# A two-layer hybrid decoder on one core: the RWKV recurrence worked in units of two pairs of heads instead of one

## Chip, core and metric

One core of a Trainium2 chip runs the whole program. The metric is the device time of one execution in microseconds (us). The engines are called as in the profile: PE (TensorE matmuls; PEld its weight loads), DVE (VectorE), ACT (ScalarE), POOL (GpSimd) and SP (SyncE, which here issues all DMAs, in order).

## The reference, cut to what matters

Two layers over 512 tokens of width 1024. Each layer projects x with one wide matrix and feeds four branches of width 512 (RWKV-7 time mixing, latent attention, a convolution module, attention into 256 memory tokens); each is gated, projected, merged with sigmoid gates, and a normalized residual closes the layer. The change lies in the RWKV branch:

```python
kk = heads(k * k_k); kk = kk / max(norm(kk), 1e-12)
k  = k * (1.0 + (a - 1.0) * k_a)
...
def step(state, inp):
    r_t, w_t, k_t, v_t, a_t, b_t = inp          # a = -kk, b = kk * a
    sa = einsum('bhvk,bhk->bhv', state, a_t)
    state = state * w_t + sa (x) b_t + v_t (x) k_t
    return state, einsum('bhvk,bhk->bhv', state, r_t)
_, y = lax.scan(step, s0, xs)                   # 512 steps, 8 heads x 64
y = (y - y_mu) * rsqrt(y_var + 64e-5) * lnx_g + lnx_b + bonus
```

## The kernel before

**Order of the work.** No order is written by hand. `Plan` (L67) keeps a clock for each engine from formulas of its own for each operation's cost, and emits the instructions in the order in which generators become due. A stream of "items" (the projections: 128-row matmuls, each product made of three from a high and a low half of both operands) is PE's main line; side tasks step in between. Tasks that wait for "small" matmuls (64 by 64) are taken together: the planner waits until GATHER (L28, 3000 ns) after the last such group, then lets every waiting small task run before it goes back to 128-row matmuls. The engines then run what was emitted, in order, waiting on semaphores for data. All engine calls go through L231, matmuls through L282, transposes through L287, DMAs through L294, so that tile names, not lines, tell the operations apart.

**Weights.** Blocks of 512 KB come by SP's queue, at most two raw ones at a time (WR); ACT rounds each half (`w..h`), DVE makes the rest (`w..l`).

**The recurrence** (`rwkv_unit`, L711). The scan is done in chunks of 64 tokens as matrix products. A unit is one pair of heads `j` (128 channels on the partitions) and one half `hf` of the 512 tokens, so four chunks for two heads: eight blocks of 64 by 64. There are 16 units, eight in each layer. The steps of a unit, by their tile names:

- `zw` (PE, 128 rows), `th`, `ta`, `cum` (scan on DVE), `kk`, `sq`, `D`, `E`, `bt`, `w`, `AR`: decays, keys and queries scaled;
- `g` (small matmuls): products of `bt` and `AR`, and the squared norms; from these `rn` and, with one scalar instruction for each of four blocks, the strictly triangular `M`; `Mc` gathers M's 16 by 16 diagonal blocks with the mask `bm`, and `moff` then clears them in M;
- `substitution()`: `Mc` goes to DRAM and comes back as `W`, one 16 by 16 block for each of 32 partitions; 30 POOL instructions invert the blocks into `ZT`; that goes to DRAM and comes back as `tc`, `zq`, `zc`;
- meanwhile `kt`, `bo` (the bonus), and `gk` (three sets of eight small matmuls, and six transposes into a second tile);
- `T`, `Zd`, `Q` spread the inverted blocks with the mask `bm` on DVE, then four small steps assemble the inverse: `x0` (needs T), `x1` (needs Zd), `x2`, `va`;
- `gb` (state updates `Gs`, `H`, and `B`, `Y0`), three `w` steps that carry the state `S` from chunk to chunk, and `yb`, the output;
- group normalization of `yb` (bn_stats, `gr` by POOL, four subtract-and-scale on DVE), transposes `ty`, and `yr`.

In the profile the digit after x is left out, so `x<-T,M` is x0 and `x<-QQ,PP` is x2.

**What overlaps.** Up to the bonus a unit may run while the unit before is still in its substitution (the conditions on `L["mids"]`, `L["toks"]`, `L["front"]`); from `gk` on, units follow each other. Two fronts, and a front and a middle, are so in flight at once, with tiles in two or three buffers. The units of a pair start when its r, k and v are there. The RWKV gate `rg` for pair i is ready when `L["units"] >= 2 * i + 2`.

Of the kernel before, what the change touches and what calls it, by code (L numbers as in the profile page):

```python
# [27 lines left out]
GATHER = 3000.0  # L28
# [18 lines left out]
for _n, _c in _PARTS:  # L47
# [6 lines left out]
    ("minc", 64), ("moff", 64), ("bm", 4), ("id2", 64),  # L54
# [148 lines left out]
class Engine:  # L203
# [5 lines left out]
    def __getattr__(self, name):  # L209
        f = getattr(self.eng, name)  # L210

        def call(*a, **k):
# [5 lines left out]
            if self.key == "ACT":  # L218
                c = (65 if isinstance(k.get("scale", 0.0), (int, float)) else 270) + 0.83 * n
            elif self.key == "POOL":  # L220
                c = 200 + 167 * n if k.get("op") == ALU.pow else 250 + 1.6 * n
            elif name == "scalar_tensor_tensor":
                c = 100 + 1.07 * n
# [38 lines left out]
def trunk_kernel(ctx: ExitStack, tc: tile.TileContext, A, out, dbg=None):  # L262
# [82 lines left out]
    scr = [[dp.tile([32 * (n + 1), 256], F32, tag=f"scr{n}{i}", name=f"scr{n}{i}").rearrange("a b -> (a b)") for n in range(2)] for i in range(2)]  # L345
# [9 lines left out]
    dpads = [cp.tile([128, 4, 65], F32, tag=f"dpad{i}", name=f"dpad{i}") for i in range(3)]  # L355
# [238 lines left out]
    def layer_items(l):  # L594
# [62 lines left out]
        def begin_rwkv(get):  # L657
# [6 lines left out]
            L["blk"] = [L["rp"].tile([32] + n, F32, tag=x, name=x + t_) for x, n in (("W", [16, 16]), ("ZT", [2, 16, 16]), ("tmpW", [56]))]  # L664
# [26 lines left out]
        def q3(ap, c=4):  # L691
            return ap.rearrange("p (c v) -> p c v", c=c)

        def rk2(tag, name, shape, bufs=1):
            return L["rp"].tile([128] + shape, F32, tag=tag, name=name, bufs=bufs)

        state = [None] * 4
        L["yr"] = [None] * 4
        L["units"] = L["chains"] = L["toks"] = L["mids"] = L["subs"] = L["next"] = L["read"] = 0
        L["front"] = False  # L700
# [8 lines left out]
        quads = [(cp, c2, h) for cp in range(2) for c2 in range(2) for h in range(2)]  # L709

        def rwkv_unit(j, hf, r, k, v):  # L711
            t = f"_{l}_{j}_{hf}"
            un = 2 * j + hf
            cs = slice(256 * hf, 256 * hf + 256)
            rr, kr, vr = r[:, cs], k[:, cs], v[:, cs]
            jc = slice(128 * j, 128 * j + 128)
            om = PRM[l][2]

            def rt(name, tag=None, dt=F32, bufs=1):
                return L["rp"].tile([128, 256], dt, tag=tag or name, name=name + t, bufs=bufs)  # L720

            def chunks(ap):

                return ap.rearrange("p (a b) w -> p b a w", b=2)

            def by2(ap):
                return ap.rearrange("p (a b) w -> p a b w", a=2)

            z, = yield from pa.take([128, 2, 256], "zw" + t)
            for i, (h, lo, x) in enumerate(L["lora"]):  # L730
                MM(z[:, i, :], h[:, jc], x[:, cs], start=True, stop=False)
                MM(z[:, i, :], lo[:, jc], x[:, cs], start=False, stop=True)
            yield
            th, ta = rt("th"), rt("ta")
            S.activation(th, z[:, 0, :], AF.Tanh, scale=0.5, bias=hp("w0", j))
            S.activation(ta, z[:, 1, :], AF.Tanh, scale=0.5, bias=hp("a0", j))
            pa.free()
            V.tensor_scalar(out=th, in0=th, scalar1=1.0, scalar2=KAPPA, op0=ALU.add, op1=ALU.mult)
            yield
            cum = rt("cum")  # L740
            V.tensor_tensor_scan(out=cum, data0=reset, data1=th, initial=0.0, op0=ALU.mult, op1=ALU.add)
            kk, sq = rt("kk"), rt("sq")
            S.activation(sq, kr, AF.Square, scale=pr("k_k", j))
            S.activation(kk, kr, AF.Copy, scale=pr("k_k", j))
            yield
            D = dpads[un % 3]
            S.activation(D[:, :, 1:65], q3(cum), AF.Exp, scale=-1.0)
            E = rt("E", "th")
            S.activation(E, cum, AF.Exp)
            yield lambda: L["toks"] >= un - 1  # L750
            bt, kt, w = rt("bt", bufs=2), rt("kt", bufs=2), rt("w")
            V.scalar_tensor_tensor(out=bt, in0=ta, scalar=1.0, in1=kk, op0=ALU.add, op1=ALU.mult)
            V.scalar_tensor_tensor(out=bt, in0=bt, scalar=0.5, in1=E, op0=ALU.mult, op1=ALU.mult)
            S.activation(w, ta, AF.Identity, scale=hp("k_a", j), bias=om[:, 13 + j:14 + j])
            yield
            yield lambda: L["mids"] >= un - 1
            AR = rk2("AR", "AR" + t, [4, 2, 64], 2)
            V.scalar_tensor_tensor(out=AR[:, :, 0, :], in0=q3(kk), scalar=-1.0, in1=D[:, :, 0:64], op0=ALU.mult, op1=ALU.mult)
            V.tensor_tensor(out=AR[:, :, 1, :], in0=q3(rr), in1=D[:, :, 1:65], op=ALU.mult)
            yield  # L760

            yield lambda: L["subs"] == un
            g0, = yield from pg.take([128, 2, 512], "g" + t, 1, "small")
            for cp, c2, h in quads:
                c = 2 * cp + c2
                MM(g0[HALF[c2], h, 64 * cp:64 * cp + 64], bt[HALF[h], 64 * c:64 * c + 64], AR[HALF[h], c, 0], start=True, stop=True, four=True)
            for cp, c2, h in quads:
                c = 2 * cp + c2
                MM(g0[HALF[c2], h, 128 + cp:129 + cp], sq[HALF[h], 64 * c:64 * c + 64], bones2[HALF[h], h:h + 1], start=True, stop=True, four=True)
            yield  # L770
            s1, rn = st("s1" + t, 4), rk2("rn", "rn" + t, [4], 3)
            V.tensor_scalar(out=s1.rearrange("p (a b) -> p a b", a=2), in0=g0[:, :, 128:130], scalar1=1e-24, scalar2=None, op0=ALU.max)
            V.reciprocal(rn[:, 0:4:2], s1[:, 0:4:2])
            V.reciprocal(rn[:, 1:4:2], s1[:, 3:0:-2])
            M = rk2("M", "M" + t, [4, 64], 2)
            for h in range(2):
                for cp in range(2):
                    e = 2 * (h ^ cp) + cp
                    V.scalar_tensor_tensor(out=M[:, e, :], in0=g0[:, h, 64 * cp:64 * cp + 64], scalar=rn[:, e:e + 1], in1=cc("mstr"), op0=ALU.mult, op1=ALU.mult)
            pg.free()  # L780
            bm = cc("bm")
            Mc = rk2("Mc", "Mc" + t, [4, 16])
            V.tensor_scalar(out=Mc, in0=M[:, :, 0:16], scalar1=bm[:, 0:1], scalar2=None, op0=ALU.mult)
            for b in range(1, 4):
                V.scalar_tensor_tensor(out=Mc, in0=M[:, :, 16 * b:16 * b + 16], scalar=bm[:, b:b + 1], in1=Mc, op0=ALU.mult, op1=ALU.add)
            V.tensor_tensor(out=M, in0=M, in1=cc("moff").unsqueeze(1).to_broadcast([128, 4, 64]), op=ALU.mult)
# [5 lines left out]
            def substitution():  # L792
# [3 lines left out]
                DMA(d1.rearrange("(c p t) -> p c t", c=4, t=16), Mc)  # L796
                plan.due(d1)
                yield
                DMA(W.rearrange("p a b -> p (a b)"), d1.rearrange("(q e) -> q e", q=32), "W" + t)
# [6 lines left out]
                for q in range(1, 15):  # L806
                    n = 15 - q
                    o = tmp[:, 0:q * n].rearrange("p (a b) -> p a b", a=q)
                    G.tensor_tensor(out=o, in0=zz[:, 0:q, q:q + 1].to_broadcast([32, q, n]),
                                    in1=W[:, q:q + 1, q + 1:16].to_broadcast([32, q, n]), op=ALU.mult)  # L810
# [6 lines left out]
                DMA(d2.rearrange("(z q e) -> q z e", z=2, q=32), ZT.rearrange("p z a b -> p z (a b)"))  # L817
                plan.due(d2)
                yield
                zc, tc_, zq = (rk2(n, n + t, [4, 16], 1 + (n != "zq")) for n in ("zc", "tc", "zq"))  # L820
                dz, dt = (d2[4 * 128 * 16 * i:4 * 128 * 16 * (i + 1)] for i in range(2))
                DMA(tc_, dt.rearrange("(e p t) -> p e t", e=4, t=16))
                DMA(zq, dz.rearrange("(e p t) -> p e t", e=4, t=16))
                dz = dz.rearrange("(h c p t) -> h p c t", h=2, c=4, t=16)
                for h in range(2):
                    DMA(zc[HALF[h]], dz[h])
# [5 lines left out]
            V.tensor_tensor(out=w, in0=w, in1=kr, op=ALU.mult)  # L832
            V.tensor_tensor(out=kt, in0=w, in1=E, op=ALU.mult)
            yield
            rbh, rbl = rt("rbh", "kk", F32R), rt("rbl", "ta", F32R)
            V.scalar_tensor_tensor(out=w, in0=rr, scalar=pr("r_k", j), in1=w, op0=ALU.mult, op1=ALU.mult)
            yield from split(rbh, rbl, w)
            yield
            bo, = yield from pa.take([128, 256], "bo" + t)
            MM(bo, bones, rbl, start=True, stop=False)  # L840
            MM(bo, bones, rbh, start=False, stop=True)
            yield
            yield lambda: L["units"] >= un - 2
            bon = rk2("bon", "bon" + t, [256], 3)
            V.tensor_tensor(out=bon, in0=bo, in1=vr, op=ALU.mult)
            pa.free()
            L["front"] = False


            yield lambda: L["mids"] == un  # L850
# [190 lines left out]
        def room():  # L1041

            return min(adds[0:8]) > 0
# [915 lines left out]
```

## Time and profile before

| | before |
|---|---|
| time, median of 3 runs | 1540.28 us (1539.13 to 1546.58) |
| the profiled execution, as timed | 1538.63 us |
| its span, first to last instruction | 1536.5 us |
| PE busy | 1508.7 us, 98% of the span |
| DVE, ACT, POOL busy | 1123.2, 650.1, 238.1 us |
| instructions, all engines | 30218 |
| DMA bytes, busy share of the 16 engines (queue q1) | 151.61 MB, 32.7% |
| granted clock of PE | 0.997 |

The profile is one execution. A row of a timeline is start, duration, engine, line, operation, output and inputs, for PE the rows by columns of the array, the moving size, and how many instructions it stands for; a 64 by 64 matmul in float32 is two of them. A row of a stretch gives its length, then the busy us (and instructions) of PE, PEld, DVE, ACT and POOL, the granted clock, the DMA share and GB/s. A group's row ends in busy us, mean ns, and the idle time before. PE's matmuls are pipelined, so the distance of two starts, not a duration, is what a matmul costs PE.

### The profile page before, as it was taken

The numbers are of one execution on the slowest core, as the hardware profiler recorded it, in microseconds if no ns is written. First come the engines' busy times: TensorE is split into PE (matmuls) and PEld (weight loads), VectorE is DVE, ScalarE is ACT, GpSimd is POOL, SyncE is SP. The second block draws the span as 40 slices with busy tenths as digits, with TensorE's granted clock in tenths as the row PEclk, the third lists the DMA queues.
The fourth block names the chain that finished last, engine by engine and source line by source line (L and its number), as shares of the span: only waits on it lengthen the run. The fifth ranks groups of instructions, "written<-read, shape, count | busy, mean of one in ns | idle before, by whom it ended". The sixth has DMA issues, their size and how long they took to land.

```text
span 1536.5 us, 30218 instructions
## 1 busy us (share of the span) xinstructions
PE 1508.7 (98%) x11912; PEld 1239.7 (81%) x11912; DVE 1123.2 (73%) x2503; ACT 650.1 (42%) x1403; POOL 238.1 (15%) x588
## 2 busy tenths in 40 slices
PE   8999999999999999999999999999999999999997
PEld 8878788877787777888998877788777777778886
DVE  5789888888657775455554888887977777745747
ACT  5546654443234332344365454534423533323332
POOL 0000000345214330000000000000534333300002
PEclk9999999999999999999999999999999999999998
DMA  6452422232322232424343243332222222326231
GB/s 207 122 163 70 117 83 83 78 89 64 90 82 78 61 96 83 147 97 137 113 154 107 80 121 91 86 110 87 76 76 76 66 77 75 95 78 205 96 113 66
DMA packets 89662, 153.54 MB, mean 100 GB/s; under 512 B 41648, under 2 KB 47792, under 8 KB 89520
## 3 DMA queue, kind: packets, MB, share of 16 engines
q1 hardware_dynamic: 89520, 151.61, 32.7%
q8 instruction: 93, 1.52, 0.4%
q14 instruction: 49, 0.40, 0.1%
HBM read 134.27 MB, written 5.77 MB: 91 GB/s over the span
## 4 chain that ended last, share of the span: by engine, by line
PE 85%; DVE 7%; DMA 3%; ACT 2%; issue 1%; POOL 0%; SPq 0%; ACTq 0%; DVEq 0%; POOLq 0%
PE ps_m L282 22%; PE po L282 11%; PE ps_cg L282 3%; PE ps_rg L282 3%; PE ps_k L282 3%; PE ps_xg L282 3%; PE ps_v L282 3%; PE ps_xq L282 3%; PE ps_r L282 3%; PE ps_mg L282 3%; PE ms L282 2%; PE ps_glu L282 2%; PE pz L282 2%; PE pl L282 2%; PE ps_val L282 2%; DMA w<-in_w_ch_dram 2%
## 5 line engine op out<-in xcount | busy, mean ns | idle before, releaser
L231 DVE SCALAR_TENSOR_TENSOR cacc<-hpad,prm,cacc 128x512 f32<-128x512 f32 x240 | 179.7, 751 | 3.3
L231 ACT ACTIVATE tm<-ps_m,prm 128x512 f32<-128x512 f32 x64 | 44.1, 689 | 135.1 <-PE ps_m L282 135.0
L231 POOL TENSOR_SCALAR ZT<-W 32x256 f32<-32x256 f32 x16 | 7.3, 457 | 562.5 <-DMA W<-scr 320.9
L231 DVE SCALAR_TENSOR_TENSOR mt<-tm,po 128x512 f32<-128x512 f32 x48 | 33.0, 687 | 77.5 <-PE po L282 77.5
L231 POOL TENSOR_TENSOR ZT<-ZT,tmpW 32x14 f32<-32x14 f32 (+6 forms) x224 | 85.1, 380 | 17.6
L231 POOL TENSOR_TENSOR tmpW<-ZT,W 32x14 f32<-32x14 f32 (+6 forms) x224 | 85.0, 379 | 15.9
L231 POOL TENSOR_SCALAR lrs<-lmv 128x1 f32<-128x1 f32 x8 | 1.7, 206 | 302.1 <-DVE lmv L231 302.1
L231 POOL TENSOR_SCALAR gr<-gm 128x4 f32<-128x4 f32 x16 | 5.5, 343 | 262.3 <-DVE gm L231 262.3
L231 ACT ACTIVATE mP<-ms,nmm 128x128 f32<-128x128 f32 (+3 forms) x64 | 33.6, 527 | 19.4 <-DVE nmm L231 16.7
L231 DVE TENSOR_TENSOR merged<-merged,mt 128x512 f32<-128x512 f32 x48 | 33.7, 702 | 1.7
L231 DVE TENSOR_REDUCE nmm<-ms 128x1 f32<-128x128 f32 (+3 forms) x64 | 30.3, 485 | 0.8 <-PE ms L282 0.3
L231 ACT COPY mPT<-mt 128x128 f32<-128x128 f32 (+3 forms) x64 | 26.2, 430 | 11.1 <-PE mt L287 10.7
L231 DVE SCALAR_TENSOR_TENSOR S<-w,dpad,H 128x64 f32<-128x64 f32 x48 | 13.5, 281 | 22.8 <-PE w L282 22.6
L287 PE MATMUL mt<-cst,mP 128*128 128x128 f32 x160 | 27.0, 277 | 1.1 <-DVE smm L231 0.7
L231 DVE TENSOR_SCALAR mP<-mP,smm 128x128 f32<-128x128 f32 (+3 forms) x64 | 24.8, 387 | 2.3
L282 PE MATMUL mo<-mPT,v 128*64 128x128 f32 x320 | 24.3, 282 | 0.0
L231 ACT ACTIVATE xP<-xs,nmx 128x256 f32<-128x256 f32 x32 | 15.2, 475 | 21.3 <-DVE nmx L231 21.0
L287 PEld LDWEIGHTS mt<-cst,mP 128*128 128x128 f32 x160 | 18.8, 141 | 6.7 <-issue 1.0
L231 ACT ACTIVATE z<-z,lnb,lrs 128x256 f32<-128x256 f32 (+1 forms) x16 | 9.6, 648 | 30.8 <-DVE lnb L231 30.8
L282 PE MATMUL ms<-kTl,qT 96*128 96x128 f32 (+3 forms) x64 | 22.5, 352 | 0.0
L282 PEld LDWEIGHTS mo<-mPT,v 128*64 128x64 f32 x320 | 16.8, 136 | 5.3 <-issue 3.1
L282 PE MATMUL ms<-kTh,qT 96*128 96x128 f32 (+3 forms) x64 | 20.6, 323 | 0.0
(3516 smaller groups left out, 5424.4 us busy)
## 6 DMA issues: line engine op xcount, KB each, us to landing
w<-in_w_ch_dram SPq DMA_DIRECT2D x146, 512.0 KB, 3.8
w<-in_w_o_dram SPq DMA_DIRECT2D x32, 512.0 KB, 3.7
w<-in_w_out_dram SPq DMA_DIRECT2D x16, 512.0 KB, 3.8
w<-in_w_lat_dram SPq DMA_DIRECT2D x16, 336.0 KB, 3.0
w<-in_w_mk_dram SPq DMA_DIRECT2D x8, 512.0 KB, 3.7
w<-in_w_mv_dram SPq DMA_DIRECT2D x8, 512.0 KB, 3.7
w<-in_w_qk_dram SPq DMA_DIRECT2D x8, 320.0 KB, 2.9
x<-in_xT_dram SPq DMA_DIRECT2D x8, 256.0 KB, 6.3
```

The source lines that it names most:

```text
L231: return self.plan.keep(f(*a, **k))
L282: plan.keep(nc.tensor.matmul(o, lhsT, rhs, start=start, stop=stop))
L287: plan.keep(nc.tensor.transpose(o, i, ident))
```

## The change

A unit becomes two neighbouring pairs of heads (s = 0, 1) and one half of the tokens: 8 units in all, four in each layer. Every step is done for both: each small step has the sets of both pairs in one go, DVE and ACT instructions take 512 columns where the operands allow (L707 to L1060 of the new kernel), the substitution has 64 partitions of blocks and transfers twice as large, `zc` in four transfers instead of two.

- A unit now begins only when the one before has passed its `gb` (`L["mids"] == un`), and `x0` waits for the previous unit's whole chain; the conditions on `toks`, `front`, `next` and the second buffers go. Early and late operands share tiles by tags (`s0` to `s5`, `T`, `Q`, `Z`, `PT`, `bt`, `kt`); `yr` is written over `r`.
- To ACT go: the affine step of `th`, `Zd` and `Q` (four activations each, with bm as scale), and the normalization of `yb` (eight activations with scale and bias, and a new small `mr` for the bias). `T` stays on DVE.
- `M` is two multiplications with `rn` broadcast instead of four instructions with a scalar; the triangular mask is put on `Mc` by the new `m16`.
- `gk`'s transposes become three steps of their own (`tk0`, `tk1`, `tk2`).
- GATHER is 2000. The planner's formulas for DVE and ACT costs are changed. The items for r, k, v, for the latent attention's heads (they wait for the memory keys), and the turn of the `mg` gates have other conditions.

Matmuls with at most 64 output rows number 2560 in the order before and in the order now; the runs of them that belong to the recurrence, unbroken by a 128-row matmul, are 130 before and 88 now.

On PE, step `va` of layer 0's first unit, before (`ps_m` are matmuls of a projection's merge gate; `va` and `x` belong to the recurrence):

```order
L282 MATMUL ps_m_0_3809<-xh_0_170,w51h_3670 128x512
L282 MATMUL ps_m_0_3809<-xh_0_170,w51l_3671 128x512
L282 MATMUL va_0_0_3808<-RA_0_0_3408,Zi_0_0_3787 64x128 x8
L282 MATMUL ps_m_0_3809<-xl_0_183,w51h_3670 128x512
L282 MATMUL ps_m_0_3809<-xh_0_182,w51h_3670 128x512
```

and now:

```order
L286 MATMUL ps_m_0_4063<-xh_0_128,w55h_3865 128x512
L286 MATMUL ps_m_0_4063<-xh_0_128,w55l_3866 128x512
L286 MATMUL va_0_0_4062<-RA_0_0_0_3682,Zi_0_0_4051 64x128 x8
L286 MATMUL va_0_0_4062<-RA_0_0_0_3683,Zi_0_0_4051 64x128 x8
L286 MATMUL ps_m_0_4063<-xl_0_154,w55h_3865 128x512
L286 MATMUL ps_m_0_4063<-xh_0_153,w55h_3865 128x512
```

A run that held one pair's eight matmuls holds both pairs' sixteen.

On SP, the substitution of layer 0's first unit among weight loads (`w`), before:

```order
L294 DMA scr_88<-Mc_0_0_3241 128x4x16
L294 DMA W_2770<-scr_88 32x256
L294 DMA w_3300<-in_w_ch_dram 128x1024
L294 DMA w_3427<-in_w_ch_dram 128x1024
L294 DMA w_3492<-in_w_ch_dram 128x1024
L294 DMA scr_89<-ZT_2771 32x2x256
L294 DMA tc_0_0_3538<-scr_89 128x4x16
L294 DMA zq_0_0_3539<-scr_89 128x4x16
L294 DMA zc_0_0_3537<-scr_89 64x4x16 x2
L294 DMA w_3546<-in_w_o_dram 128x1024
```

and now:

```order
L298 DMA scr_88<-Mc_0_0_3474 128x8x16
L298 DMA W_2891<-scr_88 64x256
L298 DMA w_3541<-in_w_ch_dram 128x1024
L298 DMA w_3568<-in_w_o_dram 128x1024
L298 DMA w_3745<-in_w_ch_dram 128x1024
L298 DMA scr_89<-ZT_2892 64x2x256
L298 DMA tc_0_0_3782<-scr_89 128x8x16
L298 DMA zc_0_0_3781<-scr_89 64x4x16 x4
L298 DMA zq_0_0_3783<-scr_89 128x8x16
L298 DMA w_3816<-in_w_ch_dram 128x1024
```

The queue's pattern is the same; the blocks of both pairs go together, and `zq` goes behind the four `zc`.

The diff, cut to its core:

```diff
-GATHER = 3000.0
+GATHER = 2000.0
...
+    ("m16", 16),
...
-    dpads = [cp.tile([128, 4, 65], ...) for i in range(3)]
+    dpads = [cp.tile([128, 8, 65], ...) for i in range(2)]
...
-        def rwkv_unit(j, hf, r, k, v):
+        def rwkv_unit(j0, hf, rkv):
+            js = list(enumerate((j0, j0 + 1)))
...
+            yield lambda: L["mids"] == un
...
-            V.tensor_scalar(out=th, in0=th, scalar1=1.0, scalar2=KAPPA, op0=ALU.add, op1=ALU.mult)
+            S.activation(th, th, AF.Copy, scale=KAPPA, bias=KAPPA)
...
-            yield lambda: L["subs"] == un
             g0, = yield from pg.take([128, 2, 512], "g" + t, 1, "small")
-            for cp, c2, h in quads:
-                c = 2 * cp + c2
-                MM(g0[HALF[c2], h, 64 * cp:64 * cp + 64], bt[HALF[h], 64 * c:64 * c + 64], AR[HALF[h], c, 0], ...)
+            for s in SUB:
+                for cp, c2, h in quads:
+                    c = 2 * cp + c2
+                    MM(g0[HALF[c2], h, 128 * s + 64 * cp:128 * s + 64 * cp + 64], bt[HALF[h], s, 64 * c:64 * c + 64], AR[HALF[h], s, c, 0], ...)
...
-            for h in range(2):
-                for cp in range(2):
-                    V.scalar_tensor_tensor(out=M[:, e, :], in0=g0[...], scalar=rn[:, e:e + 1], in1=cc("mstr"), op0=ALU.mult, op1=ALU.mult)
+            for cp in range(2):
+                V.tensor_tensor(out=M[...], in0=gm[...], in1=rn[:, :, cp:4:2].unsqueeze(3).to_broadcast([128, 2, 2, 64]), op=ALU.mult)
...
+            V.tensor_tensor(out=Mc, in0=Mc, in1=cc("m16").unsqueeze(1).to_broadcast([128, 8, 16]), op=ALU.mult)
...
-                DMA(tc_, dt.rearrange("(e p t) -> p e t", e=4, t=16))
-                DMA(zq, dz.rearrange("(e p t) -> p e t", e=4, t=16))
-                for h in range(2):
-                    DMA(zc[HALF[h]], dz[h])
+                DMA(tc_, dt.rearrange("(e p t) -> p e t", e=8, t=16))
+                for s in SUB:
+                    for h in range(2):
+                        DMA(zc[HALF[h], 4 * s:4 * s + 4], d4[s, h])
+                DMA(zq, dz.rearrange("(e p t) -> p e t", e=8, t=16))
...
-            yield lambda: L["subs"] > un
+            yield lambda: L["subs"] > un and L["chains"] == un
...
-            for dst, src in ((T, tc_), (Zd[:, 0:2], chunks(zc)[:, 0]), (Zd[:, 2:4], chunks(zc)[:, 1]), (Q, zq)):
-                V.tensor_tensor(out=dst..., in0=src..., in1=bm..., op=ALU.mult)
+            V.tensor_tensor(out=T..., in0=tc_..., in1=bm..., op=ALU.mult)
+            for x, src in ((Zd, zc), (Q, zq)):
+                for b in range(4):
+                    S.activation(x...[:, :, b], src, AF.Copy, scale=bm[:, b:b + 1])
...
-            for e in range(4):
-                V.tensor_scalar(out=yb[:, e], in0=yb[:, e], scalar1=mv[...], scalar2=rs[:, e:e + 1], op0=ALU.subtract, op1=ALU.mult)
+            for e in range(8):
+                S.activation(y8[:, e], y8[:, e], AF.Identity, scale=rs[:, e:e + 1], bias=mr[:, e:e + 1])
...
-                ch_item(..., lambda: "lora" in L and L["read"] >= j - (j == 1 or room()))
+                ch_item(..., lambda: "lora" in L and (j < 2 or L["read"] or room()))
...
-                 lambda: len(latT) == 5 and ... and L["pairs"] >= hh - 1)
+                 lambda: len(latT) == 5 and ... and L["pairs"] >= hh - 1 and MEM[l] is not None)
...
-            return n == 3 or added[{1: 3, 2: 1, 0: 2}[n]] >= 6
+            return n == 3 or added[{1: 3, 2: 1, 0: 2}[n]] >= (8 if n == 1 else 6)
...
-        gate_items(0, CH_RG, "rg", lambda i: L["units"] >= 2 * i + 2, L["yr"], Y[0], bias)
+        gate_items(0, CH_RG, "rg", lambda i: L["units"] >= 2 + i // 2 * 2, L["yr"], Y[0], bias)
```

More of the change, by code (lines that the diff above doesn't have):

```diff
@@ L689, in wlal @@
                 V.tensor_tensor(out=m[HALF[1 - h]], in0=x[HALF[h]], in1=m.bitcast(F32)[HALF[h]], op=ALU.subtract)
[L691 to L695, printed above, removed]
         state = [None] * 4
         L["yr"] = [None] * 4
-        L["units"] = L["chains"] = L["toks"] = L["mids"] = L["subs"] = L["next"] = L["read"] = 0
-        L["front"] = False
+        L["units"] = L["chains"] = L["mids"] = L["subs"] = L["read"] = 0
@@ L755, in rwkv_unit @@
             yield
[L756 to L759, printed above, removed]
+            AR = rk("AR", [2, 4, 2, 64])
+            V.scalar_tensor_tensor(out=AR.rearrange("p s c m w -> p (s c) m w")[:, :, 0, :], in0=both(kk), scalar=-1.0, in1=D[:, :, 0:64], op0=ALU.mult, op1=ALU.mult)
@@ new lines, in rwkv_unit @@
+            for s in SUB:
+                for cp, c2, h in quads:
+                    c = 2 * cp + c2
+                    MM(g0[HALF[c2], h, 256 + 2 * s + cp:257 + 2 * s + cp], sq[HALF[h], s, 64 * c:64 * c + 64], bones2[HALF[h], h:h + 1], start=True, stop=True, four=True)
+            yield
+            s1, rn = st("s1" + t, 8), rk("rn", [2, 4], bufs=2)
+            V.tensor_scalar(out=s1.rearrange("p (a b) -> p a b", a=2), in0=g0[:, :, 256:260], scalar1=1e-24, scalar2=None, op0=ALU.max)
+            s1 = s1.rearrange("p (h s c) -> p s h c", h=2, s=2)
@@ L837, in rwkv_unit @@
+            for s, j in js:
+                V.scalar_tensor_tensor(out=w[:, s], in0=rr[s], scalar=pr("r_k", j), in1=w[:, s], op0=ALU.mult, op1=ALU.mult)
             yield from split(rbh, rbl, w)
             yield
-            bo, = yield from pa.take([128, 256], "bo" + t)
-            MM(bo, bones, rbl, start=True, stop=False)
-            MM(bo, bones, rbh, start=False, stop=True)
+            bo, = yield from pa.take([128, 512], "bo" + t)
+            MM(bo, bones, rbl.rearrange("p s w -> p (s w)"), start=True, stop=False)
@@ L842, in rwkv_unit @@
+            MM(bo, bones, rbh.rearrange("p s w -> p (s w)"), start=False, stop=True)
             yield
-            yield lambda: L["units"] >= un - 2
-            bon = rk2("bon", "bon" + t, [256], 3)
-            V.tensor_tensor(out=bon, in0=bo, in1=vr, op=ALU.mult)
+            for s, j in js:
+                if hf == 0:
+                    L["yr"][j] = rkv[s]["r"]
+                V.tensor_tensor(out=rr[s], in0=bo[:, 256 * s:256 * s + 256], in1=vr[s], op=ALU.mult)
             pa.free()
-            L["front"] = False
@@ L850, in rwkv_unit @@
-            yield lambda: L["mids"] == un
-            gr, tk = yield from pg.take([128, 2, 512], "gk" + t, 2)
-            tk = tk.rearrange("p a w -> p (a w)")
-            for x, src in enumerate((bt, kt, vr)):
-                for cp in range(2):
-                    TR(tk[:, 256 * x + 128 * cp:256 * x + 128 * cp + 128], src[:, 128 * cp:128 * cp + 128])
-            yield "small"
-            gp = gr[:, :, 0:128].rearrange("p h (a w) -> p h a w", a=2)
-            gv = gr[:, :, 128:384].rearrange("p h (a w) -> p h a w", a=2)
@@ L948, in rwkv_unit @@
             yield
-            yield lambda: L["chains"] == un
-            ps, y0 = yield from pg.take([128, 2, 512], "gb" + t, 2, "small")
-            y0 = y0[:, :, 0:128].rearrange("p a (h w) -> p a h w", h=2)
-            gb = ps[:, :, 0:256].rearrange("p c (a w) -> p c a w", a=2)
-            hh = ps[:, :, 256:384].rearrange("p c (a w) -> p c a w", a=2)
-            for cp, c2, h in quads:
-                MM(gb[HALF[h], c2, cp], VA[HALF[c2], 2 * (h ^ cp) + cp, 64:128], BP[HALF[c2], 2 * h + cp], start=True, stop=True, four=True)
@@ L970, in rwkv_unit @@
[L970 to L975 removed]
+            gbs = yield from pg.take([128, 2, 512], "gb" + t, 2, "small")
@@ L984, in rwkv_unit @@
                 if hf == 0 and c == 0:
-                    states.append(H[:, 0, :])
+                    states.append([H[:, s, 0] for s in SUB])
                 elif hf == 0 or c < 3:
-                    ps, = yield from pa.take([128, 64], f"w{c}" + t, 1, "small")
-                    for half in HALF:
-                        MM(ps[half], Gs[half, e], states[c][half], start=True, stop=True)
+                    ps, = yield from pa.take([128, 2, 64], f"w{c}" + t, 1, "small")
+                    for s in SUB:
+                        for half in HALF:
+                            MM(ps[half, s], Gs[half, s, e], states[c][s][half], start=True, stop=True)
@@ L1386, in pair_item @@
             item([(A["w_qk"][l, hh], (384, 256))], run,
-                 lambda: len(latT) == 5 and len(qpe) > hh // 2 and len(vtok) == 4 and L["pairs"] >= hh - 1)
+                 lambda: len(latT) == 5 and len(qpe) > hh // 2 and len(vtok) == 4 and L["pairs"] >= hh - 1 and MEM[l] is not None)
         def heads(T, ps, n, s, there):
```

391 lines of the change are left out of this document (211 added, 180 removed).

## Prediction

> **What bounds the kernel now.** I read the busy shares of the profile's page first, then the stretches, then the timeline of TensorE (PE) in the recurrence. All times are of the profiled execution: a span of 1536.5 us, 1538.6 us as timed, 1.6 us under the median of the three runs shown. The sum is made against 1538.6.
>
> ```profile
> span 1536.5 us, 30218 instructions
> PE 1508.7 (98%) x11912; PEld 1239.7 (81%) x11912; DVE 1123.2 (73%) x2503; ACT 650.1 (42%) x1403; POOL 238.1 (15%) x588
> ```
>
> PE is idle for 27.8 us in all. Three stretches, with the busy time of PE, its weight loads, DVE, ACT and POOL in each:
>
> ```profile
> 0.00:20.00 20.00, 14.02 (x81) 14.03 (x82) 12.26 (x36) 11.16 (x20) 0.99 (x14) 1.00 0.69 232
> 300.00:400.00 100.00, 99.08 (x1256) 78.20 (x1255) 84.11 (x205) 37.48 (x82) 44.53 (x103) 1.00 0.30 82
> 1450.00:1536.50 86.50, 76.21 (x359) 63.89 (x357) 51.82 (x105) 25.07 (x44) 10.02 (x16) 0.95 0.26 86
> ```
>
> Of the 27.8 us, 6.0 lie in the first 20 us and 10.3 in the last 86.5, where the change does nothing; 11.5 are spread over the 1430 us between. In the recurrence (300 to 400) PE is busy 99%. So the time is PE's work put end to end, and an edit counts by what it takes from PE's instruction stream, or by the idle time that it opens there.
>
> What does the recurrence cost PE? Its matmuls are 64 by 64 and stand in small runs between 128-row matmuls of the projections. Two such runs of unit 0, in PE's timeline (start, duration; x16 is eight matmuls in two passes each):
>
> ```profile
> 301.44 0.39 PE L282 MATMUL ps_m<-xh,w49h 128*128 128x512 f32 x1
> 301.67 0.39 PE L282 MATMUL ps_m<-xh,w49l 128*128 128x512 f32 x1
> 301.99 0.46 PE L282 MATMUL x<-T,M 64*64 64x64 f32 x16
> 302.27 0.41 PE L282 MATMUL x<-M,T 64*64 64x64 f32 x16
> 302.50 0.41 PE L282 MATMUL x<-vt,NQ 64*64 64x64 f32 x16
> 302.85 0.50 PE L282 MATMUL ps_m<-xl,w49h 128*128 128x512 f32 x1
> 303.18 0.39 PE L282 MATMUL ps_m<-xh,w49h 128*128 128x512 f32 x1
> ...
> 310.54 0.39 PE L282 MATMUL po<-yxg1h,w50l 128*128 128x512 f32 x1
> 310.85 0.46 PE L282 MATMUL x<-QQ,PP 64*64 64x64 f32 x16
> 311.25 0.50 PE L282 MATMUL po<-yxg2l,w50h 128*128 128x512 f32 x1
> ```
>
> The large matmuls start every 0.23 us (301.44 to 301.67); the one behind a run takes 0.33 (302.85 to 303.18). From the last large one before a run to the first after it are 1.18 us with three sets of eight and 0.71 with one. Less the stride of 0.23, and with the 0.10 that the next one takes longer, the runs cost 1.05 and 0.58 us. So a set costs (1.05 - 0.58) / 2 = 0.235 us, and **a run costs 0.35 us more than what is in it**, whatever its length: going in and coming out. This is the price that the change bears on.
>
> **The change, part by part.** *Units of two pairs.* The matmuls themselves stay: 2560 with 64 output rows or fewer in the instruction order, before and now. But the order has 130 runs of the recurrence's small matmuls before and 88 now (11 for each of 8 units: g, gk, x0, x1, x2, va, gb, three w, yb). 16 units with 11 steps would be 176; the planner before already let 46 of them share a run. 42 runs at 0.35 us are **14.7 us less work for PE**. Between ends: 0.30 to 0.40 by the rounding of four starts, so 12.6 to 16.8. zw, bo and the transposes keep their columns, so they cost the same.
>
> *DVE and ScalarE.* Steps for both pairs halve the instructions, and three kinds go to ScalarE.
>
> ```profile
> L231 DVE TENSOR_SCALAR yb<-yb,gm,gr 128x64 f32<-128x64 f32 x64 | 16.1, 314 | 4.0 <-POOL gr L231 4.0
> L231 DVE SCALAR_TENSOR_TENSOR M<-g,rn,cst 128x64 f32<-128x64 f32 x64 | 13.8, 278 | 0.0
> L231 DVE TENSOR_TENSOR T<-tc,cst 128x256 f32<-128x256 f32 x16 | 6.7, 418 | 0.0
> L231 DVE TENSOR_TENSOR NQ<-gk,cst 128x512 f32<-128x512 f32 x16 | 10.9, 680 | 0.0
> L231 ACT ACTIVATE w<-ta,om,prm 128x256 f32<-128x256 f32 x16 | 9.6, 598 | 0.0
> ```
>
> DVE loses yb's 16.1 us; M's 64 instructions become 16 of T's size (13.8 to 6.7); two of 256 columns made one of 512 save 2 x 418 - 680 = 156 ns, some 70 times, 11 us. ScalarE gains 64 normalizations of 64 columns and 64 block diagonals of 128: under w's 598 ns each, so under 77 us on an engine with 886 us idle. None of it is on PE's path: cost nothing, covered by DVE's 27% and ScalarE's 58% of idle time. If the cover went (ScalarE late with Zd and Q), x1 and QQ would be late, the case below.
>
> *One unit at a time.* Now a unit starts only when the one before has its Gs and H (the count of mids), so no second front runs during the substitution. The substitution is the one long chain: Mc is written to DRAM, read back 16 by 16, solved on POOL, and comes back as tc, zc, zq. Unit 0 before:
>
> ```profile
> 269.05 0.46 PE L282 MATMUL g<-AR,bt 64*64 64x64 f32 x16
> 272.50 0.39 SPq L294 DMA_DIRECT2D scr<-Mc  x1
> 274.38 0.34 SPq L294 DMA_DIRECT2D W<-scr  x1
> 277.27 0.40 POOL L231 TENSOR_SCALAR ZT<-W 32x256 f32<-32x256 f32 x1 [232.07 <-DMA W<-scr]
> ...
> 292.15 0.34 SPq L294 DMA_DIRECT2D scr<-ZT  x1
> 294.38 0.38 SPq L294 DMA_DIRECT2D tc<-scr  x1
> ...
> 296.04 0.62 SPq L294 DMA_DIRECT2D zc<-scr  x1
> ```
>
> x0, the first matmul that needs T, started at 301.99 (above): 32.9 us after g. What the chain needs now until x0 may start: to Mc's write 3.45, and 0.4 for the second half of g, and about 0.5 for DVE's longer Mc steps and the new mask; 1.9 to W; 2.9 to POOL; 14.9 on POOL; 2.2 to tc's issue; 2.1 to its landing (row below); T itself 0.7 (NQ's 680 ns is of that size), handing over 0.3. Together **29.4 us**. It must fit between g and x0 in PE's stream. There the order now has, unit by unit, two runs with ten sets (3.1 us), 119 to 152 large matmuls, and 16 to 28 transposes at 0.11 us (two in 0.22 us, next rows):
>
> ```profile
> 280.70 0.38 PE L287 MATMUL gk_0x<-cst,bt 128*128 128x128 f32 x2
> 280.92 0.38 PE L287 MATMUL gk_0x<-cst,kt 128*128 128x128 f32 x2
> ```
>
> Shortest, the third unit of layer 0: 3.1 + 119 x 0.23 + 28 x 0.11 = 33.6. The eight are 34.1, 34.3, 33.6, 37.1 in layer 0 and 41.1, 35.7, 37.1, 38.4 in layer 1. So x0 has 4 us to spare at the least. Zd and Q come later: four issues of zc at 0.62 us and one of zq behind tc, then eight activations on ScalarE, some 5 us more; x1, which needs Zd, stands behind x0's own run of six sets (1.8 us) and some large matmuls, 3 us or more. That is nearly used up in the shortest units, so I set 2 us for small stalls there, between 0 and 8 (1 us a unit).
>
> *The DMAs.* Transfers are twice as large and half as many, behind the same weights on SP's queue; SP waits for POOL's ZT 8 times and not 16, with weight loads queued behind it each time. Size hardly shows in the landing (KB each, us):
>
> ```profile
> scr<-ZT SPq DMA_DIRECT2D x16, 64.0 KB, 1.6
> scr<-Mc SPq DMA_DIRECT2D x16, 32.0 KB, 1.8
> W<-scr SPq DMA_DIRECT2D x16, 32.0 KB, 1.7
> tc<-scr SPq DMA_DIRECT2D x16, 32.0 KB, 2.1
> ```
>
> 64 KB lands no later than 32 KB, and Mc in pieces of 64 bytes only 0.1 us later than W in pieces of 1 KB. I take no growth. Were all four landings to double, the chain would be 7.2 us longer, 36.6, and the eight units would wait 2.5, 2.3, 3.0, 0, 0, 0.9, 0, 0: 9 us, the middle case below. The Trainium skill speaks for that: by "DMA: Bandwidth & Descriptors" (Specifications) a transfer reaches line rate only in pieces of 512 bytes or more, and these have 64. The trace does not bear it out, with 0.1 us between pieces of 64 bytes and of 1 KB.
>
> The other edits (the later start of the latent attention, GATHER 2000, the gates' turn) reorder large matmuls that PE has to do anyway: nothing, or 2 us either way by the 11.5 us that PE idles in mid kernel.
>
> **Sum:** 1538.6 - 14.7 + 2 = **1526 us**.
>
> **The rivals.** *Slower: POOL's time goes with the partitions.* The substitution now covers 64 partitions, not 32. If its 14.9 us became 27, the chain would be 41.5 us, and x0 would wait 7.4, 7.2, 7.9, 4.4, 0.4, 5.8, 4.4, 3.1: 41 us, or 1565. Against it: POOL takes 0.20 us for 128x8, and the first step on 32x14, of like columns, took as little.
>
> ```profile
> 42.97 0.20 POOL L231 TENSOR_TENSOR rsl<-ssl,cst 128x8 f32<-128x8 f32 x1 [41.39 <-ACT jk L231]
> 277.81 0.21 POOL L231 TENSOR_TENSOR tmpW<-ZT,W 32x14 f32<-32x14 f32 x1
> ```
>
> It decides from a substitution of 24.4 us in every unit, where the chain is 38.9 us and the stalls, 22 us, eat the gain and 0.5% more. Chance 0.10.
>
> *No change: DVE holds POOL up.* Two substitutions before, the fastest and the slowest:
>
> ```profile
> 454.90:467.10 12.20, 12.20 (x103) 10.19 (x102) 7.35 (x16) 8.31 (x19) 9.83 (x31) 1.00 0.34 128
> 1136.50:1158.80 22.30, 21.05 (x262) 16.73 (x261) 18.50 (x48) 8.79 (x21) 13.96 (x38) 1.00 0.17 54
> ```
>
> 12.2 us where DVE is 60% busy, 22.3 where it is 83%. With 22.3 in all units the chain is 36.8 us, and x0 waits 2.7, 2.5, 3.2, 0, 0, 1.1, 0, 0: 10 us, so 1534 (stalls of 7 to 22 us from whatever cause are this case). By "SBUF — State Buffer" of the Trainium skill (Who interferes with whom) a DVE instruction with two SBUF inputs locks out a GpSimd one that reads SBUF for its whole length, and those of this chain double in length. For the case: the rows; against: DVE has some 34 us less to do. Chance 0.18.
>
> *More: the lighter DVE gives back half of the 11.5 us of idle PE and no stall comes:* 1518. Chance 0.12. *The forecast* (0 to 7 us of stalls): 0.60.
>
> **The numbers.** About 0.5%, 7.7 us, is what a measurement of this kernel can tell from no change. Faster: 0.60 + 0.12 = 0.72; within: 0.18; slower: 0.10. The range runs from 1517 (the upper case, and 1 us for the run's price) to 1539 (the middle case's stalls up to 15 us): it leaves out the slow case and the end of the middle one.
>
> **What would show it.** Right: 42 fewer runs and about 15 us less busy PE; x0's T in no long wait of PE; idle PE still near 28 us; POOL about half as busy. A single run of two sets should cost 0.35 + 0.47 us. Wrong: PE waiting at x for DVE T or ScalarE Z, some us in each unit; POOL's instructions on 64 partitions longer than on 32; or runs whose price grows with their length, so that fewer runs save nothing.

## The result and the profile after

The changed kernel takes 1525.22 us (median of 4 runs, 1523.32 to 1526.59) against 1540.01 us for the kernel before beside it: a ratio of 0.9894, 95% interval 0.9865 to 0.9923. In a second measurement (run 9 below) it was 0.9895, 0.9880 to 0.9910. The forecast was 1526 us. The profiled execution took 1526.59 us, 12.0 less than that of before; the sum on record had 12.7.

The busy shares on the page of the kernel after:

```profile
span 1524.8 us, 29673 instructions
PE 1494.6 (98%) x11896; PEld 1240.3 (81%) x11896; DVE 1064.7 (70%) x2215; ACT 693.7 (45%) x1515; POOL 134.8 (9%) x323
```

PE's busy time fell by 14.1 us and its idle time rose from 27.8 to 30.2 us: 11.7 us less span. That is the whole change of time. Of the busy time after, some 1.7 us come from a stretch of 3.4 us at half the granted clock (0.50 from 898.9 to 902.3), half of its length by estimate. The profile before has no such stretch while PE works, and run 9's, of the same kernel as after, has none either: there PE is busy 1492.4 us, 16.3 less than before. The three stretches that were shown of before, now:

```profile
0.00:20.00 20.00, 13.82 (x74) 13.82 (x75) 12.37 (x36) 11.35 (x21) 0.97 (x13) 1.00 0.70 233
300.00:400.00 100.00, 98.74 (x1081) 80.04 (x1080) 71.16 (x154) 45.70 (x103) 29.44 (x72) 1.00 0.29 79
1438.30:1524.80 86.50, 76.27 (x360) 63.95 (x358) 51.88 (x105) 25.07 (x45) 10.01 (x16) 0.95 0.26 85
```

The two ends are as before (6.2 and 10.2 us of idle PE), the middle has 13.8 us where it had 11.5. The x2 step of the second unit, in PE's timeline:

```profile
410.88 0.39 PE L286 MATMUL ps_r<-xh,w64l 128*128 128x512 f32 x1
411.19 0.69 PE L286 MATMUL x<-QQ,PP 64*64 64x64 f32 x32
411.82 0.50 PE L286 MATMUL ps_r<-xl,w64h 128*128 128x512 f32 x1
412.16 0.39 PE L286 MATMUL ps_r<-xh,w64h 128*128 128x512 f32 x1
```

From 410.88 to 411.82 are 0.94 us; less the stride of 0.23, and with the 0.11 that the next large matmul takes longer, a run of two sets costs 0.82 us. The forecast was 0.35 + 0.47. Before, two such sets stood in two runs of 0.58.

PE's waits after (us in total, times, longest), the two longest and those in the recurrence:

```profile
PE pl L286 <- DVE w0l L235: 6.2, 1, 6.2
PE pq L286 <- DVE xql L235: 2.6, 2, 1.6
...
PE gb_1x L286 <- issue: 1.5, 1, 1.5
...
PE gb_0x L286 <- issue: 0.5, 1, 0.5
PE x L286 <- DVE PP L235: 0.5, 1, 0.5
PE w L286 <- DVE yc L235: 0.5, 1, 0.5
PE x L286 <- ACT RA L235: 0.2, 1, 0.2
```

None is a wait of x0 for T or of x1 for Zd. The substitution of the second unit, from g to x0:

```profile
367.47 0.69 PE L286 MATMUL g<-AR,bt 64*64 64x64 f32 x32
...
376.71 0.40 POOL L235 TENSOR_SCALAR ZT<-W 64x256 f32<-64x256 f32 x1 [6.93 <-DMA W<-scr]
...
390.36 0.62 SPq L298 DMA_DIRECT2D scr<-ZT  x1
...
395.14 0.69 DVE L235 TENSOR_TENSOR T<-tc,cst 128x512 f32<-128x512 f32 x1
...
401.97 0.46 PE L286 MATMUL x<-T,M 64*64 64x64 f32 x16
```

T is ready 28.4 us after g (forecast 29.4 to x0, with 0.3 for handing over), and x0 starts 34.5 us after g (34.3 by the instructions between them). In the eight units x0 starts 34.3, 34.5, 34.1, 37.2, 41.3, 35.9, 37.1 and 38.6 us after g, each within 0.5 us of the prediction's list.

### The profile page after: what moved, and what is told of

Its sections match the earlier page's. It is cut to its first block, busy times and chain, and to the rows that moved or that the text cites. A ratio compares the mean times of both kernels' runs of the same rounds, so it can differ in the third digit from the quotient of the medians.

```text
span 1524.8 us, 29673 instructions
## 1 busy us (share of the span) xinstructions
PE 1494.6 (98%) x11896; PEld 1240.3 (81%) x11896; DVE 1064.7 (70%) x2215; ACT 693.7 (45%) x1515; POOL 134.8 (9%) x323
## 4 chain that ended last, share of the span: by engine, by line
PE 89%; DVE 4%; DMA 3%; ACT 2%; SPq 1%; issue 1%; POOL 0%; ACTq 0%; POOLq 0%; DVEq 0%
PE ps_m L286 22%; PE po L286 11%; PE ps_cg L286 3%; PE ps_k L286 3%; PE ps_mg L286 3%; PE ps_r L286 3%; PE ps_v L286 3%; PE ps_rg L286 3%; PE ps_xg L286 3%; PE ps_xq L286 2%; PE ps_val L286 2%; PE ms L286 2%; PE pz L286 2%; PE pl L286 2%; PE ps_glu L286 2%; DMA w<-in_w_ch_dram 2%
## 5 line engine op out<-in xcount | busy, mean ns | idle before, releaser
L235 POOL TENSOR_TENSOR ZT<-ZT,tmpW 64x14 f32<-64x14 f32 (+6 forms) x112 | 43.4, 388 | 8.8
L235 POOL TENSOR_TENSOR tmpW<-ZT,W 64x14 f32<-64x14 f32 (+6 forms) x112 | 40.9, 365 | 8.0
L235 POOL TENSOR_SCALAR ZT<-W 64x256 f32<-64x256 f32 x8 | 4.3, 533 | 324.6 <-DVE mo L235 260.0
L235 ACT ACTIVATE yb<-yb,mr,gr 128x64 f32<-128x64 f32 x64 | 22.1, 430 | 5.9 <-DVE mr L235 5.9
L235 ACT ACTIVATE z<-z,lnb,lrs 128x256 f32<-128x256 f32 (+1 forms) x16 | 9.6, 647 | 29.4 <-DVE lnb L235 29.4
```

What stands on the lines that cost most here:

```text
L235: return self.plan.keep(f(*a, **k))
```

## The experiments

The theory: the gain is 42 fewer runs of small matmuls at 0.35 us of PE time. The rivals: the lighter DVE and POOL brought it, or the new order of the large matmuls did. A second question was how much room the substitution has left.

**1. Every run cut in two.** The first `for s in SUB` loop of the steps g, gk, x0, x1, x2, va, gb, w and yb gets

```diff
 for s in SUB:
+    if s:
+        yield lambda: plan.cut == (128, 128)
     for cp, c2, h in quads:
```

> The kernel after, with every run of small matmuls of the recurrence cut in two, and a large matmul between the two pairs' halves: 176 runs in the order where the kernel after has 88. The matmuls, DVE's, ScalarE's and POOL's instructions and the DMAs are those of the kernel after. Theory (a run costs TensorE 0.35 us, whatever is in it): 88 x 0.35 = 31 us more busy PE than after, so 1525 + 31 = 1556 us, slower than the kernel before (130 runs) by 16 us, that is 46 x 0.35. Rival (the gain came from fewer and wider instructions on DVE and POOL and from ScalarE's share): these are all kept, so 1525 us. Rival (the gain came from the new order of the large matmuls): kept as well, 1525 us.

(x1, which has two products, falls into three runs, and in eight places a half of yb or w stands with a half of the next unit's g: 176 in all.)

Measured: 1563.46 us, ratio to before 1.0157 (1.0143 to 1.0171): 38 us more than after, with DVE, ACT and POOL unchanged (1064.5, 693.1, 134.0 us busy).

```profile
PE 1531.0 (98%) x11896; PEld 1242.1 (79%) x11896; DVE 1064.5 (68%) x2215; ACT 693.1 (44%) x1515; POOL 134.0 (9%) x323
```

x2 of layer 0's first unit there, in PE's timeline:

```profile
347.46 0.39 PE L286 MATMUL ps_m<-xh,w55l 128*128 128x512 f32 x1
347.78 0.46 PE L286 MATMUL x<-QQ,PP 64*64 64x64 f32 x16
348.17 0.50 PE L286 MATMUL ps_m<-xl,w55h 128*128 128x512 f32 x1
348.51 0.39 PE L286 MATMUL ps_m<-xh,w55h 128*128 128x512 f32 x1
...
349.06 0.46 PE L286 MATMUL x<-QQ,PP 64*64 64x64 f32 x16
```

Each half costs (348.17 - 347.46) - 0.23 + 0.11 = 0.59 us, together 1.18 where the joint run costs 0.82: 0.36 for the run more. PE is busy 36.4 us longer, 0.41 for each of the 88; of the 5 us above 88 x 0.36, 1.7 are one stretch of 3.4 us at half clock more than after has (202.3 and 1431.1, 0.50 each), and 3 I have not accounted for. Both rivals say 1525, and fall as the main cause: all that they count on is in this kernel.

**2. The kernel before, gathered more.** `GATHER = 4500.0` in place of 3000.

> The kernel before with one number of its planner changed: small matmuls are held back until 4.5 us, not 3, of large ones have passed, so more of them stand together. The order has 139 runs of small matmuls in all (the memory attention's among them) where before has 161; each pair of heads still has units of its own. Theory (0.35 us a run): 22 x 0.35 = 7.7 us less, 1532 us, if no step of a chain comes late by it. Rival (wider instructions on DVE and POOL, or the larger transfers, brought the gain): 1540 us, none of them is in it.

Measured: 1541.45 us, ratio 1.0006 (0.9998 to 1.0015). The theory's 7.7 us did not come. The waits and the stretch near the end show why (waits as above; stretches with PE, PEld, DVE, ACT, POOL, then the granted clock):

```profile
PE ty L287 <- DVE yb L231: 4.4, 1, 4.4
PE w L282 <- DVE S L231: 2.7, 2, 1.5
```

```profile
1414.00:1420.00 6.00, 1.64 (x22) 0.97 (x21) 2.89 (x14) 0.60 (x1) 1.20 (x2) 0.84 0.89 220
1420.00:1425.00 5.00, 5.00 (x14) 3.87 (x14) 2.93 (x7) 0.62 (x1) 0.00 (x0) 0.51 1.02 346
```

In the last unit no large matmul stands between yb and ty in PE's stream, and PE waited 4.4 us. Then the clock was at half for some 5 us more. PE's idle time is 33.2 us (27.8 before), and its busy time is what it was, 1508.6: the mean granted clock is 0.993 against 0.997, worth about 6 us of busy time. But this execution took 1544.05 us; the median of the eleven, 1541.45 us, had a clock of 0.997, that of before. So the clock alone does not hide the 7.7 us. The waits, 5.4 us more, can eat most of it; the rest is open, as there is no profile of the median execution. The price of a run isn't refuted here, but neither does this run show it.

**3. The new order, in part.** The kernel before with two conditions and the planner's costs of the change (the costs aren't shown).

```diff
-... and L["pairs"] >= hh - 1)
+... and L["pairs"] >= hh - 1 and MEM[l] is not None)
-return n == 3 or added[{1: 3, 2: 1, 0: 2}[n]] >= 6
+return n == 3 or added[{1: 3, 2: 1, 0: 2}[n]] >= (8 if n == 1 else 6)
...
```

> The kernel before with only those edits of the change that order the large matmuls: the latent attention waits for the memory, the gates of the attention wait for 8 merges, and the planner has the new costs for ScalarE and DVE. 160 runs of small matmuls, before has 161; units of one pair of heads. Theory (the runs): 1540 us within 2 us. Rival (the order of the large matmuls brought the gain): 1525 to 1530 us.

Measured: 1540.08 us, ratio 1.0000 (0.9989 to 1.0011). These three edits by themselves are worth nothing. The new conditions for r, k and v and GATHER 2000 are not among them; run 11 tests GATHER.

**4. ScalarE's share put back on DVE.**

```diff
-for b in range(4):
-    S.activation(x...[:, :, b], src, AF.Copy, scale=bm[:, b:b + 1])
+V.tensor_tensor(out=x..., in0=src..., in1=bm..., op=ALU.mult)
...
-S.activation(y8[:, e], y8[:, e], AF.Identity, scale=rs..., bias=mr...)
+V.tensor_scalar(out=y8[:, e], in0=y8[:, e], scalar1=mv..., scalar2=rs..., op0=ALU.subtract, op1=ALU.mult)
```

> The kernel after with the work that it moved to ScalarE put back on DVE: the group normalization (64 instructions of 64 columns), the block diagonals Z and Q (16 of 512 columns in place of 64 activations) and the decay's scaling. 88 runs as after. DVE has some 30 us more to do, mainly in the recurrence. Theory (runs; DVE and ScalarE are covered): 1525 us within 2 us. Rival (the gain comes from the relief of DVE): a part of the 15 us is lost, 1530 to 1540 us.

Measured: 1527.86 us, ratio 0.9919 (0.9905 to 0.9932). DVE is busy 1091.2 us (1064.7), PE idle 30.6 us (30.2). Against after the difference is 2 to 3 us by the medians and some 4 us by the ratios, with intervals that meet: the move to ScalarE is worth some 4 us at most by these medians and ratios, or nothing, not the 15.

**5. The kernel before, not gathered.** `GATHER = 0.0`.

> The kernel before with the planner's number at 0: it no longer holds small matmuls back so that they stand together. 158 runs of the recurrence's small matmuls where before has 130, and one more of the memory attention's; units, instructions and transfers of before. Theory (0.35 us a run): 29 x 0.35 = 10 us more, 1550 us; no chain gets later by it. Rival (the price of a run is small where units are of one pair, and the gain of the change came from the wider units): 1540 us.

Measured: 1553.19 us, ratio 1.0092 (1.0074 to 1.0110), 14 us more. PE is busy 10.7 us longer, 0.37 us for each of the 29 runs; 1.7 us of that lie in a stretch of 3.4 us at half clock (0.50 from 1194.2 to 1197.6), which before has not, and without them it is 0.31:

```profile
PE 1519.4 (98%) x11912; PEld 1243.4 (80%) x11912; DVE 1124.0 (73%) x2503; ACT 650.6 (42%) x1403; POOL 241.5 (16%) x588
```

So a price near 0.35 holds in units of one pair, with the units, instructions and transfers of before.

**6 and 7. A later substitution.** 14 (48) times in each unit, into a scratch tile that the substitution then overwrites:

```diff
+for _ in range(14):
+    plan.keep(nc.gpsimd.tensor_tensor(out=tmp[:, 0:8], in0=zz[:, 0, 0:8], in1=W[:, 0, 0:8], op=ALU.mult))
 G.memset(zz.rearrange("p a b -> p (a b)")[:, 0:256:17], 1.0)
```

> The kernel after with 14 more multiplications of 64x8 on POOL ahead of each unit's substitution, into a scratch tile, in no plan: at 0.20 us each (128x8 before) the substitution ends 2.8 us later. Theory (x0 has 3.4 to 9 us to spare, from the landing of tc to x0 in the trace of after; T's later start there is DVE's queue): no change, 1525 us within 2 us. Rival (T ends as late as the chain lets it, 0.3, 6.1, 2.9, 4.9, 2.7, 3.3, 1.4 and 0.8 us ahead of x0's weights in the eight units): waits of 2.5, 1.4 and 2.0 us and some tenths, 1531 us.

> The kernel after with 48 such multiplications on POOL in each unit, 9.6 us. Theory (spare 3.4, 5.8, 5.0, 5.6, 4.6, 6.2, 6.9 and 9.0 us in the eight units by the landings of tc): TensorE waits 6 + 4 + 5 + 4 + 5 + 3 + 3 + 1 = 31 us at x0 for T, 1556 us, and more if the clock falls behind such waits. By the prediction's own chain of 29.4 us the waits are 22 us, 1547 us. Rival (the substitution is off the path, so nothing waits): 1525 us.

Measured: 1549.26 us, ratio 1.0065 (1.0048 to 1.0082), and 1631.49 us, 1.0598 (1.0580 to 1.0615). The delay was larger than I meant: an instruction of 0.20 us starts every 0.345 us when the next one writes the same tile.

```profile
386.96 4.83 POOL L817 TENSOR_TENSOR tmpW<-ZT,W 64x8 f32<-64x8 f32 x14
```

So 4.8 us, and 17.3 us with 48 (from 393.0 to 410.3 in the second unit). Even so, 24 us for 4.8 us in each of eight units is more than x0's room allows. PE's waits with 14:

```profile
PE x L286 <- ACT RA L235: 13.0, 8, 2.9
...
PE x L286 <- DVE T L235: 3.0, 2, 2.2
```

x0 waits for T 3.0 us; x1 waits 13.0, in all eight units. (The wait ends with RA, ScalarE's last copy out of x0's result; it follows the copy of P.) Layer 0's first unit there, on ScalarE and on the DMA queue:

```profile
336.88 1.28 ACT L235 ACTIVATE Z<-zc,cst 128x128 f32<-128x128 f32 x4 [7.69 <-DMA zc<-scr]
339.08 1.28 ACT L235 ACTIVATE Q<-zq,cst 128x128 f32<-128x128 f32 x4 [0.93 <-DMA zq<-scr]
340.40 0.62 ACT L235 CAST w55h<-w 128x512 fp32r<-128x512 f32 x1
342.46 0.62 ACT L235 CAST w56h<-w 128x512 fp32r<-128x512 f32 x1 [1.44 <-DMA w<-in_w_o_dram]
342.99 0.36 ACT L235 COPY P<-x 128x256 f32<-128x256 f32 x1
```

```profile
329.72 0.68 SPq L298 DMA_DIRECT2D scr<-ZT  x1
332.23 0.38 SPq L298 DMA_DIRECT2D tc<-scr  x1
332.65 2.57 SPq L298 DMA_DIRECT2D zc<-scr  x4
335.26 0.60 SPq L298 DMA_DIRECT2D zq<-scr  x1
335.97 0.53 SPq L298 DMA_DIRECT2D w<-in_w_ch_dram  x1
```

x1 reads P. ScalarE copies P only behind Z, Q and the rounding of two weight blocks (w55h, w56h), and those weights are issued behind the unit's own transfers. With 48, PE's idle time is 111.4 us, and its busy time 22.3 us longer, at a mean granted clock of 0.967. The waits are 52.3 us for T in six units, in the other two 10.8 us for ScalarE's tm (behind a weight that lands late) and 9.7 us for DVE's rbl (behind cn, which waits for a step that POOL takes in the middle of the substitution), and 8.2 us at x1. The prediction's own chain, 17.3 us longer, gives 8 x 17.3 less the eight spares (56.2 us) = 82 us of waits ahead of x0; they were 73, and 81 with x1's. Chain and distances were about right; where small delays bite first was not.

**8. After, gathered more.** `GATHER = 4500.0` in place of 2000.

> The kernel after with the planner's number at 4.5 us and not 2: 102 runs of small matmuls in all where after has 120, since some of the state's steps stand with the next unit's first step. Theory: 18 x 0.35 = 6.3 us less busy TensorE, 1519 us, if no step comes late; what the kernel before showed with 4.5 us (waits of 5.4 us more, and a slower clock behind them) says that most of it is lost: 1519 to 1526 us. Rival (runs cost nothing): 1525 us and no less busy TensorE.

Measured: 1530.71 us, ratio 0.9937 (0.9924 to 0.9950): slower than after by some 5 us, which neither theory allowed.

```profile
PE ty L291 <- ACT yb L235: 6.7, 6, 5.5
```

```profile
1394.00:1407.00 13.00, 4.86 (x101) 3.24 (x90) 5.34 (x30) 3.91 (x11) 1.84 (x2) 0.67 0.76 253
1407.00:1412.00 5.00, 5.00 (x13) 3.89 (x13) 4.81 (x12) 1.86 (x4) 0.00 (x0) 0.50 0.01 3
```

As in run 2: the end of the last unit stands alone (8 us of idle PE from 1394 to 1407), and five more at half clock. PE is busy 2.3 us less, at 0.993 against 0.996.

**9. After again**, unchanged: the standard for runs 10 to 12.

> The kernel after, unchanged, on the chip of the three runs beside it, so that small differences between these and it can be told. 1525 us by all theories.

Measured: 1525.91 us, ratio 0.9895 (0.9880 to 0.9910).

**10. Run 6 with Z and Q on DVE** (the first half of run 4's edit).

> The kernel with 14 more multiplications on POOL in each unit (1549 us), with the block diagonals Z and Q on DVE again, two instructions of 512 columns in place of 64 activations in all. Theory (x1 waits in all eight units because P's copies stand on ScalarE behind Z and Q, which wait for zc to land): P is copied as soon as x0 is done, the 13.0 us of waits at x1 fall to a few, and 1549 us to 1530 to 1540 us; what is left is T's own lateness and the later weight loads behind the substitution on the DMA queue. Rival (x1 waits since zc itself lands too late): Zd is as late on DVE, and the time stays at 1549 us within 3 us.

Measured: 1558.13 us, ratio 1.0103 (1.0087 to 1.0120). Both theories fail: it got slower, with 19.6 us of waits at x1. Layer 0's first unit, on ScalarE:

```profile
341.65 0.62 ACT L235 CAST w55h<-w 128x512 fp32r<-128x512 f32 x1 [11.90 <-DMA w<-in_w_ch_dram]
...
343.43 0.36 ACT L235 COPY P<-x 128x256 f32<-128x256 f32 x1
```

Z and Q are gone from ScalarE, and P is as late. In this unit P's copy follows the issue of the weight behind the unit's transfers by 6.78 us in after (328.02 to 334.80), 7.02 in run 6 (335.97 to 342.99) and 6.93 here (336.50 to 343.43). So the weight decides there, not Z, Q or zc. In the other seven units of run 10 it is the same: ScalarE waits 3.7 to 10.3 us for a weight block to land, and copies P about 0.5 to 1.1 us after it starts to round it. P's copy starts 10.7 to 13.2 us after ZT is written to DRAM, in run 6 10.8 to 13.3. Run 10 is slower mainly by the 6.6 us that x1 waits longer: in its order x0 stands up to 3.3 us closer behind that write. Weights issued ahead, or rounded behind P, weren't tried.

**11 and 12. Toward a faster kernel.** After with `GATHER = 3000.0`, and after with 4500 but 2000 in the last unit of each layer (set where a unit starts).

> The kernel after with the planner's number back at 3 us: 114 runs in all where after has 120, since yb and w of a unit stand with g of the next in six places. Theory: 6 x 0.35 = 2.1 us less, 1523 us, if nothing comes late by it. Rival (the waits that it brings eat it, as with 4.5 us): 1525 to 1528 us.

> The kernel after with the planner's number at 4.5 us, but 2 us in the last unit of each layer, where the trace of the kernel with 4.5 us throughout waits 5.5 us at ty and 2 us at w, with no large matmul left to put there, and then runs eleven large matmuls at half the clock. 112 runs in all where after has 120. Theory: 8 x 0.35 = 2.8 us less and no such wait, 1522 us. Rival (holding back costs as much elsewhere): 1525 us and more.

Measured: 1523.90 us, ratio 0.9886 (0.9871 to 0.9901), and 1529.61 us, 0.9927 (0.9913 to 0.9941). Six runs fewer give 2 us by the medians, as forecast, but the interval holds after's, so no gain is shown. The twelfth fails: its last unit waits 6.1 us at ty all the same, and it comes late: its g starts at 1332.4 us, in after at 1304.6. That the units held back ahead of it are the reason is likely, not shown. I found no version that is measurably faster than after.

## Why the prediction was right

- *42 runs at 0.35 us, 14.7 us.* Right: 14.1 us less busy PE, and about 16 (0.38 a run) without the stretch at half clock. The price was found again at 0.36 (run 1, by rows; 0.41 in sum) and 0.37 (run 5, in sum; 0.31 without its stretch at half clock). The page "TensorEngine Tiling (Array Packing)" of the Trainium skill (Key Properties) says that a change of the tiling mode drains TensorE; it names no price, and no run here tells a drain from another cause.
- *DVE and ScalarE cost nothing.* Right to within some 4 us (run 4). The size was off: DVE lost 58.5 us, not 34, since I had counted M, yb and the merging but not Z and Q (7.8 and 6.7 us on DVE before) and the decay's scaling (5.4).
- *Stalls of 2 us.* The amount was right (2.4 us more idle PE) by luck, for the place was not: x1 waits 0.2 us; the longest in the recurrence are 2.0 us in gb, with no releaser in the trace. All waits in the recurrence are 3.2 us, before 2.6; most of the rise lies elsewhere (ps_val waits 2.1 us, before 0.4).
- *x0 has 4 us to spare.* Nearly: with 4.8 us more it waits 3.0 us in sum. *x1's room is nearly used up:* right (13.0 us with 4.8 more), but for a wrong reason. I named Zd and Q; P waits on ScalarE behind weights, in all eight units when Z and Q are taken off ScalarE (run 10). The prediction saw weight loads queued on SP behind ZT and gave that no price.
- *No growth in the landings.* Wrong. Median us from issue to landing now:

```profile
scr<-ZT SPq DMA_DIRECT2D x8, 128.0 KB, 2.4
scr<-Mc SPq DMA_DIRECT2D x8, 64.0 KB, 2.2
W<-scr SPq DMA_DIRECT2D x8, 64.0 KB, 2.1
tc<-scr SPq DMA_DIRECT2D x8, 64.0 KB, 2.2
```

  Together 1.7 us a unit more than before (1.6, 1.8, 1.7, 2.1), not the 7.2 of the middle case. The chain still came out at its forecast, as POOL took 13.7 us in that unit where I had 14.9.
- *The slower rival.* POOL's first step takes what it took on 32 partitions, 0.21 us:

```profile
307.04 0.21 POOL L235 TENSOR_TENSOR tmpW<-ZT,W 64x14 f32<-64x14 f32 x1
```

  POOL's busy time went from 238.1 to 134.8 us. *The middle case:* the eight substitutions took 12.6 to 18.8 us on POOL, short of its 22.3.
- *Other edits 0.* Right for those that run 3 holds; the others weren't tested alone, but for GATHER (run 11: no difference shown between 2000 and 3000).

## What to carry to other kernels

Where TensorE is busy nearly throughout and its stream mixes array shapes, count the switches of shape from the order: here each stay in the 64 by 64 shape cost some 0.35 us (0.31 to 0.41 by the different sums) over what was done in it, so two units' work in one stay is a gain. The gain lasts as long as nothing comes late: holding work back (runs 2, 8, 12) saved 22, 18 and 8 switches, and waits at the end of the chain, with a slower clock behind them, ate all or most of the gain. Room on a chain is measured by making it later, and what bites first may be an engine's queue (here weights ahead of P on ScalarE) that the chain's own arithmetic doesn't hold.

## What was not expected of the hardware

A wait of TensorE can cost more than its length. After a wait of 4.36 us in run 2, the large matmuls started every 0.43 us and not every 0.23, for eleven of them:

```profile
1419.26 0.83 PE L287 MATMUL ty<-cst,yb 128*128 128x128 f32 x2 [4.36 <-DVE yb L231]
...
1420.74 0.63 PE L282 MATMUL ps_m<-xh,w218l 128*128 128x512 f32 x1
1421.16 0.63 PE L282 MATMUL ps_m<-xl,w218h 128*128 128x512 f32 x1
```

Run 7's 81 us of added idle time came with 22 us of added busy time, run 6's 20 with 7. "TensorE: Matmul & The Clock Gate" of the Trainium skill (Part 1: The HAM clock gate) describes this: half the clock after an idle window of about 3.4 us, and the full clock after as long a busy one. The stretch shown with run 2 agrees (0.51 over 5 us). But a wait of 1.5 us can be enough as well, and its length alone doesn't tell: in after a wait of 1.50 us at xo was followed by 3.4 us at half clock, in run 9, the same kernel, a wait of 1.50 us at the same matmul by none (1.00 from 895 to 905). In run 2 PE waited that long up to 379.3, and the clock was 0.50 soon after:

```profile
377.00:380.50 3.50, 2.00 (x44) 1.64 (x43) 2.70 (x6) 2.75 (x7) 0.00 (x0) 0.99 0.08 28
380.50:383.50 3.00, 3.00 (x8) 2.32 (x8) 2.36 (x7) 1.19 (x2) 0.43 (x2) 0.50 0.00 0
```
